# Attention's products with the values in a hybrid decoder layer: two parts of the values held stationary, two parts of the probabilities streamed

## The chip, the cores and the metric

The kernel runs on one core of a Trainium2 chip. A core has a matrix engine (TensorE, PE in the profile, with its weight loads listed as PEld), a vector engine (VectorE, DVE), a scalar engine (ScalarE, ACT), a general engine (GpSimd, POOL) and a sync engine (SyncE, SP) that here issues nearly all DMA transfers. Each engine has its own instruction queue and works through it in order; they wait for one another by semaphores. SBUF is the working memory, 128 partitions wide, and PSUM the memory into which TensorE writes its results. The metric is the device time of one execution in microseconds (us).

## The reference, cut to what matters

The layer projects the input, runs a gated linear recurrence and a sliding-window attention on the projections, merges both, and ends in a mixture of experts. The change touches the attention alone: 1024 tokens in 8 blocks of 128, 8 query heads and 2 key/value heads of width 64, a window of 128, a linear penalty on distance and one sink logit per head.

```
scores = einsum('bnqhgd,bnkhd->bnhgqk', qb, kb) * scale
logits = where(valid, scores - alibi, NEG_INF)        # own block and the block before
probs  = softmax(concatenate([logits, sink_col], -1), -1)[..., :-1]
out    = einsum('bnhgqk,bnkhd->bnqhgd', probs, vb)
```

Because the window is as wide as a block, each query sees exactly 128 keys: key c of its own block where c is not after the query, and key c of the block before where it is. The kernel therefore keeps one 128 x 128 table per head and block, filled from the one block or the other by a triangular mask.

## The kernel before, in words

All large products are float32 made of three products of a faster type (fp32r): an operand is split into a rounded part and the remainder (`split`, L96 to L98: ScalarE copies, VectorE subtracts), and `mm3` (L100 to L104) adds high x high, high x low and low x high. Attention's scores use two such products per head, since both parts of the queries lie on the two halves of the partitions (L337, L338). Its turning of the probabilities (L367), its products with the values (L381, L383) and the turning of its output (L406) use plain float32.

The work stands in stages. `att_proj` projects queries, keys and values. Then `weave` (L241) lays the pieces of `attention()` between the products of `stream()`, the remaining projections: 164 nominal us of projections are divided evenly by the number of attention's pieces, and that many products are fed before each piece. TensorE's order is this program order, fixed by `pe_order`; the other engines are ordered by the scheduler of the language. The next stage weaves the recurrence with the rest of the projections in the same manner, then come mixing and routing, and then the experts, whose weights SyncE fetches into a ring of buffers from the end of the mixing on.

For block n and half g of the heads (four heads), attention has three pieces, put into the list by the numbers in `groups` so that one group's pieces stand four places apart:

- `scores(n, g)`: eight products into the bank `sc`; ScalarE copies the own block's part (L341), VectorE overwrites the masked part from the block before (L345), adds the distance term (L350), takes the maximum (L352); ScalarE takes the exponentials (L360). `prep(n + 1)` is issued within the second group.
- `turn(n, g)`: four transposes into a bank `pa`; VectorE multiplies the result by the mask of the own block into `apc` (L369) and by the mask of the block before into `app` (L373).
- `values(n, g)`: per head `apc` is stationary and the values of the block stream, 64 columns and a 65th of ones that gives the sum of the exponentials (L381); for n > 0 the same with `app` and the block before (L383). VectorE adds the sink (L385), inverts (L386), and scales into `ob` (L387).

A fourth piece per block, `out(n)`, turns the block's output by four transposes (L406), copies it on ScalarE (L408) and stores it to DRAM (L409). The tiles named in `S2` (L68) share one ring of `n2` = 15 buffers, and the banks `mm` (3), `sc` (1) and `pa` (3) hold all of PSUM.

Of the kernel before, what the change touches and what calls it, by code (L numbers as in the profile page):

```python
# [5 lines left out]
F32 = mybir.dt.float32  # L6
F32R = mybir.dt.float32r
I32 = mybir.dt.int32
AF = mybir.ActivationFunctionType
# [51 lines left out]
class Builder:  # L61
# [3 lines left out]

    S2 = {"ob", "as", "apc", "app", "oT", "hq", "hk", "hl", "hv", "hg", "hkd", "hkT", "hqb", "hst", "hE", "hS", "hsq", "ho",  # L68
          "rxT", "rlT", "hh", "hth", "htl"}
    NQ = 36  # L70
    NX = 9
# [6 lines left out]
    def tile(self, shape, dt, tag, bufs, name=None):  # L78
        name = name or tag
        if tag in self.S2:  # L80
            tag, bufs = "s2", self.n2
# [160 lines left out]
    def att_proj(self):  # L242
        nc = self.nc
        self.xh, self.xl = [], []
        x0 = [self.load_x(0, 0)]
        raw = [self.wload_half(2048, 0)]
        x0.append(self.load_x(0, 1))
        raw.append(self.wload_half(2048, 1))
        x0 += [self.load_x(0, j) for j in (2, 3)]
        x1 = [self.load_x(1, j) for j in range(4)]  # L250
        raw2 = self.wload(2304)
        self.setup_more()
        raw3 = self.wload(2560)
        self.aq = [self.q4([128, 4, 256], name=f"aq{i}") for i in range(4)]

        def keep(ps, ch, ct, half):
            for b in range(2):
                nc.scalar.activation(self.aq[2 * half + b][:, 2 * ch + ct], ps[:, 256 * b:256 * b + 256], AF.Copy, scale=0.125)

        def query(w, ch, half):  # L260
            for ct in range(2):
                keep(self.run(self.proj_T(w, ct, half)), ch, ct, half)

        def first():

            w, xs = [], self.split_x(0, x0)
            gens = [self.proj_T(w, ct, 0) for ct in range(2)]
            for j in range(4):
                next(xs)
                if j % 2 == 0:  # L270
                    w.append(self.wsplit_half(raw[j // 2]))
                for _ in range(2):
                    for gen in gens:
                        next(gen)
            for ct, gen in enumerate(gens):
                keep(self.run(gen), 0, ct, 0)
            return w

        w = first()
        for _ in self.split_x(1, x1):  # L280
            pass
        query(w, 0, 1)
        w = self.wsplit(raw2)
        for half in range(2):
            query(w, 1, half)
        w = self.wsplit(raw3)
        self.ak = self.q4([128, T], name="ak")
        self.av = self.tile([128, 8, 2, 65], F32, "av", 1)
        nc.gpsimd.memset(self.av[:, :, :, 64:65], 1.0)
        self.ksh = self.tile([128, 2, 2, 128], F32R, "ksh", 1)  # L290
        self.ksl = self.tile([128, 2, 2, 128], F32R, "ksl", 1)
        vts = []
        for half in range(2):
            s = slice(half * 512, half * 512 + 512)
            ps = self.run(self.proj_T(w, 0, half))
            nc.scalar.copy(self.ak[:, s], ps)
            ps = self.run(self.proj_T(w, 1, half))
            vt = self.st2()
            nc.scalar.copy(vt, ps)
            vts.append(vt)  # L300
        for half, vt in enumerate(vts):
            tp = self.bank("pa", (128, 4, 128))
            for i in range(4):
                nc.tensor.transpose(tp[:, i], vt[:, i * 128:i * 128 + 128], self.c("ident"))
            nc.vector.tensor_copy(self.av[:, 4 * half:4 * half + 4, :, 0:64], tp.rearrange("p i (g d) -> p i g d", g=2))

    def attention(self):

        nc = self.nc
        lo, hi = slice(0, 64), slice(64, 128)  # L310
        V = {}

        def prep(n):
            o = (n % 2) * 128
            q = self.aq[n // 2]
            qs = self.tile([128, 2, 4, 128], F32R, "aqs", 2)
            nc.scalar.copy(qs[lo, 0], q[lo, :, o:o + 128])
            nc.scalar.copy(qs[hi, 1], q[hi, :, o:o + 128])
            nc.vector.tensor_sub(qs[hi, 0], q[lo, :, o:o + 128], qs[lo, 0].bitcast(F32))
            nc.vector.tensor_sub(qs[lo, 1], q[hi, :, o:o + 128], qs[hi, 1].bitcast(F32))  # L320
            cs = n % 2
            kb = slice(n * 128, n * 128 + 128)
            for g, own, other in ((0, lo, hi), (1, hi, lo)):
                nc.scalar.copy(self.ksh[own, g, cs], self.ak[own, kb])
                nc.scalar.copy(self.ksh[other, g, cs], self.ak[own, kb])
                for to in (own, other):
                    nc.vector.tensor_sub(self.ksl[to, g, cs], self.ak[own, kb], self.ksh[own, g, cs].bitcast(F32))
            V["qs", n] = qs
            V["ob", n] = self.tile([128, 8, 64], F32, "ob", 2)

        def scores(n, g):
            qs = V["qs", n]
# [6 lines left out]
            s = self.tile([128, 4, 128], F32, "as", 2)  # L339
# [8 lines left out]
            if g == 1 and n < 7:  # L348
                prep(n + 1)
# [4 lines left out]
            sk = self.tile([128, 4], F32, "ask", 2)  # L354
            nc.vector.tensor_sub(sk, self.sink[:, g::2], m)
            nm = self.tile([128, 4], F32, "anm", 2)
            nc.vector.tensor_scalar(nm, m, -1.0, None, op0=ALU.mult)
            nc.scalar.activation(sk, sk, AF.Exp)
            for i in range(4):
                nc.scalar.activation(s[:, i], s[:, i], AF.Exp, bias=nm[:, i:i + 1])  # L360
            V["s", n, g] = s, sk

        def turn(n, g):
            s, _ = V["s", n, g]
            pt = self.bank("pa", (128, 4, 128))
            for i in range(4):
                nc.tensor.transpose(pt[:, i], s[:, i], self.c("ident"))  # L367
            pc = self.tile([128, 4, 128], F32, "apc", 2)
            nc.vector.tensor_mul(pc, pt, self.c("le")[:, None, :].to_broadcast([128, 4, 128]))  # L369
            pp = None  # L370
            if n:
                pp = self.tile([128, 4, 128], F32, "app", 2)
                nc.vector.tensor_mul(pp, pt, self.c("gt")[:, None, :].to_broadcast([128, 4, 128]))  # L373
            V["p", n, g] = pc, pp

        def values(n, g):
            _, sk = V.pop(("s", n, g))
            pc, pp = V.pop(("p", n, g))
            o_ps = self.bank("pa", (128, 4, 65))
            for i in range(4):  # L380
                nc.tensor.matmul(o_ps[:, i], pc[:, i], self.av[:, n, i // 2], start=True, stop=not n)  # L381
                if n:
                    nc.tensor.matmul(o_ps[:, i], pp[:, i], self.av[:, n - 1, i // 2], start=False, stop=True)  # L383
            den = self.tile([128, 4, 1], F32, "ad", 2)
            nc.vector.tensor_add(den, o_ps[:, :, 64:65], sk[:, :, None])  # L385
            nc.vector.reciprocal(den, den)  # L386
            nc.vector.tensor_mul(V["ob", n][:, g::2], o_ps[:, :, 0:64], den.to_broadcast([128, 4, 64]))  # L387

        def out(n):
            self.out_T(V.pop(("ob", n)).rearrange("p h d -> p (h d)"), self.obd, n, "pa")  # L390

        prep(0)
        groups = []
        for n in range(8):
            for g in range(2):
                at = 8 * n + 4 * g
                groups += [(at, lambda n=n, g=g: scores(n, g)), (at + 5.5, lambda n=n, g=g: turn(n, g)),
                           (at + 10.6, lambda n=n, g=g: values(n, g))]
            groups.append((8 * n + 18.7, lambda n=n: out(n)))
        return [fn for _, fn in sorted(groups, key=lambda t: t[0])]  # L400

    def out_T(self, src, dst, n, tag):
        nc = self.nc
        ps = self.bank(tag, (128, 4, 128))
        for k in range(4):
            nc.tensor.transpose(ps[:, k], src[:, k * 128:k * 128 + 128], self.c("ident"))  # L406
        t = self.tile([128, 4, 128], F32, "oT", 3)
        nc.scalar.copy(t, ps)  # L408
        nc.sync.dma_start(dst.rearrange("k p t -> p k t")[:, :, n * 128:n * 128 + 128], t)  # L409


    def hg_consts(self):
# [1000 lines left out]
    def build(self):  # L1413
        pool = self.tc.tile_pool
        with pool(name="base", bufs=1) as self.base, pool(name="dr", bufs=1, space=DRAM) as self.dr:
            self.setup()
            self.n2 = 15
            self.banks = {"mm": 3, "sc": 1, "pa": 3}
            with pool(name="sb1", bufs=1, reuse_waits="tile") as self.sb, \
                    pool(name="ps1", bufs=1, space=PSUM, reuse_waits="tile") as self.ps, self.pe_order():  # L1420
# [6 lines left out]
            with pool(name="sb2", bufs=1, reuse_waits="tile") as self.sb, \  # L1427
                    pool(name="ps2", bufs=1, space=PSUM, reuse_waits="tile") as self.ps, self.pe_order():
                groups = self.hgrn()
# [58 lines left out]
```

## Time and profile before

Three runs took 1441.64, 1442.16 and 1442.84 us; the median is 1442.16. The profiled execution took 1442.8 us, of which the span from the first to the last instruction is 1441.0 us.

| stretch (us) | work | PE busy | DVE busy | ACT busy | POOL busy | DMA share |
|---|---|---|---|---|---|---|
| 80 to 306 | attention between projections | 226.00 of 226 | 130.40 | 102.36 | 0.52 | - |
| 306 to 420 | recurrence begins | 113.18 of 114 | 75.99 | 48.94 | 7.37 | 0.44 |
| 530 to 640 | recurrence ends, mixing begins | 107.99 of 110 | 69.68 | 35.50 | 22.87 | 0.55 |
| 640 to 760 | mixing and routing | 118.56 of 120 | 77.60 | 23.32 | 4.65 | 0.54 |
| 900 to 1050 | experts | 150.00 of 150 | 135.53 | 120.93 | 34.88 | 0.99 |

Busy time of PE is the time in which at least one matmul was in flight; their durations overlap, so what one costs is read from the distance between starts, not from its duration. A wait listed with an engine is idle time that ended when the named instruction was done.

### The profile page before, as it was taken

How to read it: one execution, taken by the hardware profiler on the slowest of the kernel's cores; microseconds unless marked ns; L12 is line 12 of the kernel's file. 1: busy time of each engine (PE TensorE's matmuls, PEld its weight loads, DVE VectorE, ACT ScalarE, POOL GpSimd, SP SyncE). 2: the span in 40 equal slices, each digit the busy share in tenths (PEclk: the TensorE clock that was granted, in tenths of full speed). 3: DMA queues.
4: the chain of work that ended last, by engine and by line, in shares of the span. 5: the costliest groups of instructions: out<-in, count | busy, mean ns of one | idle time of the engine just before them, and what ended most of it. 6: DMA issues, size and time to landing. Idle time of an engine off the chain costs nothing. (4 is left out here: it accounts for less than half of the span.)

```text
span 1441.0 us, 20557 instructions
## 1 busy us (share of the span) xinstructions
PE 1378.0 (96%) x7314; PEld 1147.4 (80%) x7314; DVE 1017.3 (71%) x1624; ACT 774.9 (54%) x1192; POOL 198.1 (14%) x133
## 2 busy tenths in 40 slices
PE   7999999999999999999999999999999999999844
PEld 5888899998888888788787888888888888888721
DVE  4266644646765764767746799999999999999635
ACT  4366434324443442422201688888888888888533
POOL 0000000000000000320001112222222222222123
PEclk9999999999999999999999999999999999999967
DMA  6123322344334232774466799999999999999962
GB/s 261 50 99 126 102 74 81 103 131 137 109 103 140 89 109 71 244 256 140 160 235 234 288 359 366 367 357 356 355 355 359 354 355 356 367 359 360 369 268 95
DMA packets 142555, 327.71 MB, mean 227 GB/s; under 512 B 18614, under 2 KB 59702, under 8 KB 142448
## 3 DMA queue, kind: packets, MB, share of 16 engines
q1 hardware_dynamic: 132800, 308.78, 59.4%
q0 software_dynamic: 9648, 17.57, 4.8%
q8 instruction: 59, 0.97, 0.3%
q14 instruction: 48, 0.39, 0.1%
HBM read 291.43 MB, written 52.43 MB: 239 GB/s over the span
## 5 line engine op out<-in xcount | busy, mean ns | idle before, releaser
L98 DVE TENSOR_TENSOR el<-er,eh 128x1024 fp32r<-128x1024 f32 x368 | 436.8, 1223 | 52.8 <-ACT eh L97 35.8
L97 ACT CAST eh<-er 128x1024 fp32r<-128x1024 f32 x368 | 369.2, 1053 | 99.4 <-PE mm L103 80.0
L102 PE MATMUL mm<-xh,wh 128*128 128x512 f32 x480 | 199.0, 415 | 8.3 <-ACT wh L97 7.3
L102 PE MATMUL mm<-eh,xh 128*128 128x512 f32 x496 | 196.4, 396 | 0.0
L103 PE MATMUL mm<-el,xh 128*128 128x512 f32 x496 | 196.2, 395 | 0.0
L104 PE MATMUL mm<-eh,xl 128*128 128x512 f32 x496 | 196.1, 395 | 0.0
L104 PE MATMUL mm<-xh,wl 128*128 128x512 f32 x480 | 189.1, 394 | 0.0
L103 PE MATMUL mm<-xl,wh 128*128 128x512 f32 x480 | 188.4, 393 | 0.8 <-DVE xl L98 0.8
L104 PEld LDWEIGHTS mm<-eh,xl 128*128 128x128 f32 x496 | 93.2, 188 | 22.6
L103 PEld LDWEIGHTS mm<-el,xh 128*128 128x128 f32 x496 | 93.2, 188 | 22.3
L102 PEld LDWEIGHTS mm<-eh,xh 128*128 128x128 f32 x496 | 93.2, 188 | 22.3
L102 PEld LDWEIGHTS mm<-xh,wh 128*128 128x128 f32 x480 | 91.1, 190 | 24.1 <-ACT wh L97 7.3
L104 PEld LDWEIGHTS mm<-xh,wl 128*128 128x128 f32 x480 | 90.7, 189 | 20.5 <-DVE wl L98 0.8
L103 PEld LDWEIGHTS mm<-xl,wh 128*128 128x128 f32 x480 | 91.2, 190 | 15.9 <-DVE xl L98 1.3
L102 PE MATMUL mm<-eh,hth 128*128 128x512 f32 x240 | 100.2, 417 | 0.0
L1054 POOL DMA_INDIRECT xg<-x1d,gi x32 | 58.0, 1811 | 282.8 <-PE pb L1117 266.8
L104 PE MATMUL mm<-eh,htl 128*128 128x512 f32 x240 | 94.8, 395 | 0.0
L103 PE MATMUL mm<-el,hth 128*128 128x512 f32 x240 | 94.8, 395 | 0.0
L1058 POOL DMA_INDIRECT zd<-y,gi x29 | 71.0, 2447 | 158.0 <-ACT y L1208 158.0
L102 PE MATMUL mm<-wh,xh 128*128 128x256 f32 x256 | 74.1, 290 | 0.0
L103 PE MATMUL mm<-wl,xh 128*128 128x256 f32 x256 | 72.4, 283 | 0.0
L104 PE MATMUL mm<-wh,xl 128*128 128x256 f32 x256 | 72.3, 282 | 0.0
(249 smaller groups left out, 2490.6 us busy)
## 6 DMA issues: line engine op xcount, KB each, us to landing
er<-w_g SPq DMA_DIRECT2D x128, 512.0 KB, 12.4
er<-w_u SPq DMA_DIRECT2D x128, 512.0 KB, 12.5
er<-w_d SPq DMA_DIRECT2D x128, 512.0 KB, 12.1
wr<-w_in SPq DMA_DIRECT2D x38, 512.0 KB, 4.1
gated<-st SPq DMA_DIRECT2D x32, 256.0 KB, 2.1
st<-gated SPq DMA_DIRECT2D x32, 256.0 KB, 3.3
xr<-xt SPq DMA_DIRECT2D x8, 512.0 KB, 8.9
wab<-w_a SPq DMA_DIRECT2D x16, 256.0 KB, 3.9
```

The costliest lines, as they stand in the source:

```text
L97: self.nc.scalar.copy(hi, src)
L98: (eng or self.nc.vector).tensor_sub(lo, src, hi.bitcast(F32))
L102: mm(out, lh, rh, start=start, stop=False)
L103: mm(out, lh, rl, start=False, stop=False)
L104: mm(out, ll, rh, start=False, stop=stop)
L1054: self.nc.gpsimd.indirect_dma_start(to, None, rows, bass.IndirectOffsetOnAxis(ap=self.column(self.gi, e), axis=0), bounds_check=T - 1, oob ...
L1058: self.nc.gpsimd.indirect_dma_start(self.zd, bass.IndirectOffsetOnAxis(ap=idx, axis=0), y, None, bounds_check=T - 1, oob_is_err=False, com ...
```

## The change

The values are kept in two parts, rounded and remainder, side by side: 64 columns of the one and 64 of the other make a stationary operand of 128 columns per block and key/value head. The probabilities are divided by their sum before they are turned; that sum is gathered by the exponentials themselves (`accum_out`). `turn` splits the turned probabilities into two parts, and for n > 0 masks each part for the own block on VectorE into a new tile and for the block before on GpSimd in place. In `values` the two heads of one key/value head stream together, 256 columns, in two parts. The result has the product with the rounded values on partitions 0 to 63 and that with their remainder on 64 to 127; ScalarE copies the latter down and VectorE adds. It then already has the layout that `out` made by transposes, so `out` goes, and attention has 48 pieces where it had 56. The ring `s2` has 13 buffers.

```diff
-        self.av = self.tile([128, 8, 2, 65], F32, "av", 1)
-        nc.gpsimd.memset(self.av[:, :, :, 64:65], 1.0)
+        self.av = self.tile([128, 8, 2, 2, 64], F32R, "av", 1)
...
-            nc.vector.tensor_copy(self.av[:, 4 * half:4 * half + 4, :, 0:64], tp.rearrange("p i (g d) -> p i g d", g=2))
+            av = self.av[:, 4 * half:4 * half + 4]
+            self.split(av[:, :, :, 0], av[:, :, :, 1], tp.rearrange("p i (g d) -> p i g d", g=2))
...
             nc.scalar.activation(sk, sk, AF.Exp)
+            den = self.tile([128, 4], F32, "ad", 2)
             for i in range(4):
-                nc.scalar.activation(s[:, i], s[:, i], AF.Exp, bias=nm[:, i:i + 1])
-            V["s", n, g] = s, sk
+                nc.scalar.activation(s[:, i], s[:, i], AF.Exp, bias=nm[:, i:i + 1], accum_out=den[:, i:i + 1])
+            nc.vector.tensor_add(den, den, sk)
+            nc.vector.reciprocal(den, den)
+            nc.vector.tensor_mul(s, s, den[:, :, None].to_broadcast([128, 4, 128]))
+            V["s", n, g] = s
...
-            pc = self.tile([128, 4, 128], F32, "apc", 2)
-            nc.vector.tensor_mul(pc, pt, self.c("le")[:, None, :].to_broadcast([128, 4, 128]))
-            pp = None
+            parts = [self.tile([128, 4, 128], F32R, nm, 2) for nm in ("aph", "apl")]
+            self.split(*parts, pt)
+            V["p", n, g] = [(n, parts)]
             if n:
-                pp = self.tile([128, 4, 128], F32, "app", 2)
-                nc.vector.tensor_mul(pp, pt, self.c("gt")[:, None, :].to_broadcast([128, 4, 128]))
-            V["p", n, g] = pc, pp
+                le, gt = (self.c(nm)[:, None, :].to_broadcast([128, 4, 128]) for nm in ("le", "gt"))
+                own = [self.tile([128, 4, 128], F32R, nm, 2) for nm in ("ach", "acl")]
+                for p, to in zip(parts, own):
+                    nc.vector.tensor_mul(to, p.bitcast(F32), le)
+                    nc.gpsimd.tensor_mul(p, p.bitcast(F32), gt)
+                V["p", n, g] = [(n, own), (n - 1, parts)]
...
-            o_ps = self.bank("pa", (128, 4, 65))
-            for i in range(4):
-                nc.tensor.matmul(o_ps[:, i], pc[:, i], self.av[:, n, i // 2], start=True, stop=not n)
-                if n:
-                    nc.tensor.matmul(o_ps[:, i], pp[:, i], self.av[:, n - 1, i // 2], start=False, stop=True)
-            den = self.tile([128, 4, 1], F32, "ad", 2)
-            nc.vector.tensor_add(den, o_ps[:, :, 64:65], sk[:, :, None])
-            nc.vector.reciprocal(den, den)
-            nc.vector.tensor_mul(V["ob", n][:, g::2], o_ps[:, :, 0:64], den.to_broadcast([128, 4, 64]))
-
-        def out(n):
-            self.out_T(V.pop(("ob", n)).rearrange("p h d -> p (h d)"), self.obd, n, "pa")
+            o_ps = self.bank("pa", (128, 4, 128))
+            todo = [(b, p) for b, parts in V.pop(("p", n, g)) for p in parts]
+            for j in range(2):
+                for k, (b, p) in enumerate(todo):
+                    nc.tensor.matmul(o_ps[:, 2 * j:2 * j + 2], self.av[:, b, j], p[:, 2 * j:2 * j + 2],
+                                     start=k == 0, stop=k == len(todo) - 1)
+            if g == 0:
+                V["o", n] = self.tile([128, 4, 128], F32, "oT", 3)
+            o = V["o", n][hi if g else lo]
+            low = self.tile([128, 4, 128], F32, "ob", 2)[lo]
+            nc.scalar.copy(low, o_ps[hi])
+            nc.vector.tensor_add(o, o_ps[lo], low)
+            if g:
+                self.store_T(V.pop(("o", n)), self.obd, n)
...
-            groups.append((8 * n + 18.7, lambda n=n: out(n)))
...
-            self.n2 = 15
+            self.n2 = 13
```

On TensorE, the first values piece of block 1 (`mm` is a bank of the projections, `pa` the bank of the result) stands in the order of before as

```order
L381 MATMUL pa_1016<-av_395,apc_879 128x65
L383 MATMUL pa_1016<-av_395,app_881 128x65
L381 MATMUL pa_1016<-av_395,apc_879 128x65
L383 MATMUL pa_1016<-av_395,app_881 128x65
L381 MATMUL pa_1016<-av_395,apc_879 128x65
L383 MATMUL pa_1016<-av_395,app_881 128x65
L381 MATMUL pa_1016<-av_395,apc_879 128x65
L383 MATMUL pa_1016<-av_395,app_881 128x65
L102 MATMUL mm_1006<-xh_204,wh_591 128x512
```

and in that of the change, whose lines from the attention on carry other numbers, as

```order
L104 MATMUL mm_1075<-xh_204,wl_596 128x512
L389 MATMUL pa_1085<-ach_928,av_395 128x256
L389 MATMUL pa_1085<-acl_929,av_395 128x256
L389 MATMUL pa_1085<-aph_924,av_395 128x256
L389 MATMUL pa_1085<-apl_925,av_395 128x256
L389 MATMUL pa_1085<-ach_928,av_395 128x256
L389 MATMUL pa_1085<-acl_929,av_395 128x256
L389 MATMUL pa_1085<-aph_924,av_395 128x256
L389 MATMUL pa_1085<-apl_925,av_395 128x256
L102 MATMUL mm_1075<-xh_204,wh_595 128x512
```

Eight products stand for eight, but 256 columns of the fast type for 65 of float32; the four rows `L406 MATMUL pa<-const,ob` per block have no successor.

On VectorE, around the scores of a later group (`as` is the table of scores, `am`, `ask`, `anm`, `ad` are columns of four, `st` belongs to a projection), before has

```order
L345 COPY_PREDICATED as<-const,sc 128x256 x2
L350 TENSOR_TENSOR as<-as,alibi 128x512
L352 TENSOR_REDUCE am<-as 128x4
L369 TENSOR_TENSOR apc<-pa,const 128x512
L353 TENSOR_TENSOR am<-am,sink 128x4
L373 TENSOR_TENSOR app<-pa,const 128x512
L357 TENSOR_SCALAR anm<-am 128x4
L462 TENSOR_SCALAR st_996<-st_996,om,lb 128x512
L385 TENSOR_TENSOR ad<-pa,ask 128x4
L355 TENSOR_TENSOR ask<-sink,am 128x4
L386 RECIPROCAL ad<-ad 128x4
L387 TENSOR_TENSOR ob<-pa,ad 128x4x64
```

and the change has

```order
L351 TENSOR_REDUCE am<-as 128x4
L352 TENSOR_TENSOR am<-am,sink 128x4
L354 TENSOR_TENSOR ask<-sink,am 128x4
L356 TENSOR_SCALAR anm<-am 128x4
L361 TENSOR_TENSOR ad<-ad,ask 128x4
L362 RECIPROCAL ad<-ad 128x4
L363 TENSOR_TENSOR as<-as,ad 128x512
L98 TENSOR_TENSOR apl<-pa,aph 128x512
L379 TENSOR_TENSOR ach<-aph,const 128x512
L379 TENSOR_TENSOR acl<-apl,const 128x512
L472 TENSOR_SCALAR st_1065<-st_1065,om,lb 128x512
L396 TENSOR_TENSOR oT<-pa,ob 64x512
```

The turn's work (`apl`, `ach`, `acl`) now stands behind the sum and the scaling (L361 to L363) of the group after it, where the two masks stood among the small steps before.

On GpSimd, which before had one fill (`av`) up to the recurrence's fill of `hst`, the change begins with

```order
L380 ISA
L380 TENSOR_TENSOR aph<-aph,const 128x512
L380 TENSOR_TENSOR apl<-apl,const 128x512
L380 TENSOR_TENSOR aph<-aph,const 128x512
L380 TENSOR_TENSOR apl<-apl,const 128x512
```

and has 28 of these masks, two for each of 14 groups.

## Rows read from the trace of the kernel before

**Rows 1.** The page: busy time and share of the span, TensorE.

```profile
PE 1378.0 (96%) x7314; PEld 1147.4 (80%) x7314; DVE 1017.3 (71%) x1624; ACT 774.9 (54%) x1192; POOL 198.1 (14%) x133
```

**Rows 2.** Busy time in 14 us stretches: stretch, its length, then each engine, clock, DMA.

```profile
94.40:108.80 14.40, 14.40 (x77) 12.23 (x76) 10.79 (x25) 10.72 (x25) 0.00 (x0) 1.00 0.39 131
...
236.00:250.00 14.00, 14.00 (x121) 14.00 (x120) 3.08 (x10) 4.14 (x13) 0.00 (x0) 1.00 0.18 57
...
sum 226.00, PE 226.00 PEld 209.79 DVE 130.40 ACT 102.36 POOL 0.52; mean PE 14.12 PEld 13.11 DVE 8.15 ACT 6.40 POOL 0.03
```

**Rows 3.** Waits of TensorE, 60 to 640 us: who waited, total us, times, longest.

```profile
PE mm L104 <- DVE l L98: 1.3, 3, 0.5
PE mm L102 <- ACT st L497: 0.7, 1, 0.7
PE pb L539 <- DMA hq<-hqd: 0.5, 1, 0.5
PE pb L573 <- DVE hE L559: 0.3, 1, 0.3
PE pa L304 <- ACT st L299: 0.2, 1, 0.2
```

**Rows 4.** Timeline of TensorE, a values piece of block 3: start, duration, line, operation.

```profile
180.13 0.34 PE L381 MATMUL pa<-av,apc 128*128 128x65 f32 x2
...
182.16 0.40 PE L103 MATMUL mm<-xl,wh 128*128 128x512 f32 x1
182.39 0.39 PE L104 MATMUL mm<-xh,wl 128*128 128x512 f32 x1
```

**Rows 5.** Timeline of TensorE, the turned output of block 2.

```profile
184.66 0.60 PE L406 MATMUL pa<-const,ob 128*128 128x128 f32 x4
...
185.33 0.39 PE L103 MATMUL mm<-xl,wh 128*128 128x512 f32 x1
```

**Rows 6.** Timeline of TensorE, a values piece of block 0.

```profile
98.88 1.00 PE L381 MATMUL pa<-av,apc 128*128 128x65 f32 x8
...
100.01 0.40 PE L103 MATMUL mm<-xl,wh 128*128 128x512 f32 x1
```

**Rows 7.** Timeline of TensorE, a scores piece: eight products of 256 columns.

```profile
188.52 0.28 PE L337 MATMUL sc<-ksh,aqs 128*128 128x256 f32 x1
...
189.48 0.39 PE L102 MATMUL mm<-xh,wh 128*128 128x512 f32 x1
```

**Rows 8.** Groups by line, 80 to 310 us: operands, count, busy us, mean ns, idle before.

```profile
L350 DVE TENSOR_TENSOR as<-as,alibi 128x512 f32<-128x512 f32 x16 | 11.1, 692 | 0.5
...
L369 DVE TENSOR_TENSOR apc<-pa,const 128x512 f32<-128x512 f32 x16 | 11.0, 684 | 0.7 <-PE pa L367 0.7
...
L387 DVE TENSOR_TENSOR ob<-pa,ad 128x256 f32<-128x256 f32 x16 | 6.8, 424 | 0.5
...
L408 ACT COPY oT<-pa 128x512 f32<-128x512 f32 x8 | 4.7, 587 | 23.0 <-PE pa L406 23.0
```

**Rows 9.** Line 1286, ScalarE's read of an accumulated sum: durations min/median/max in ns.

```profile
L1286 ACT ACTIVATION_READ_ACCUMULATOR w<-z x8: 185/187/198, 1386.6 to 1414.1; 128x1 f32 x8
```

**Rows 10.** Timeline of GpSimd at 582 us: one subtraction of 1024 columns.

```profile
582.70 2.40 POOL L98 TENSOR_TENSOR l<-wo,h 128x1024 fp32r<-128x1024 f32 x1 [15.31 <-PE mm L104]
```

**Rows 11.** Timeline of VectorE at the same time.

```profile
582.72 0.69 DVE L786 TENSOR_TENSOR st<-st,mm 128x512 f32<-128x512 f32 x1 [0.57 <-PE mm L104]
583.44 2.20 DVE L787 TENSOR_TENSOR st<-st,st 128x512 f32<-128x512 f32 x1
```

**Rows 12.** Timeline of ScalarE: exponentials of the first group and of the fourth.

```profile
85.77 1.28 ACT L360 ACTIVATE as<-as,anm 128x128 f32<-128x128 f32 x4
...
110.42 1.28 ACT L360 ACTIVATE as<-as,anm 128x128 f32<-128x128 f32 x4 [0.34 <-DVE anm L357]
```

**Rows 13.** Timeline of TensorE: the turns of the same two groups.

```profile
88.09 0.60 PE L367 MATMUL pa<-const,as 128*128 128x128 f32 x4
...
118.79 0.60 PE L367 MATMUL pa<-const,as 128*128 128x128 f32 x4
```

More of the change, by code (lines that the diff above doesn't have):

```diff
@@ L61 @@
 class Builder:
-    S2 = {"ob", "as", "apc", "app", "oT", "hq", "hk", "hl", "hv", "hg", "hkd", "hkT", "hqb", "hst", "hE", "hS", "hsq", "ho",
+    S2 = {"ob", "as", "aph", "apl", "ach", "acl", "oT", "hq", "hk", "hl", "hv", "hg", "hkd", "hkT", "hqb", "hst", "hE", "hS", "hsq", "ho",
           "rxT", "rlT", "hh", "hth", "htl"}
@@ L328, in prep @@
             V["qs", n] = qs
-            V["ob", n] = self.tile([128, 8, 64], F32, "ob", 2)
         def scores(n, g):
@@ L358, in scores @@
             nc.scalar.activation(sk, sk, AF.Exp)
+            den = self.tile([128, 4], F32, "ad", 2)
             for i in range(4):
-                nc.scalar.activation(s[:, i], s[:, i], AF.Exp, bias=nm[:, i:i + 1])
-            V["s", n, g] = s, sk
+                nc.scalar.activation(s[:, i], s[:, i], AF.Exp, bias=nm[:, i:i + 1], accum_out=den[:, i:i + 1])
[3 more added lines that the diff above has]
+            V["s", n, g] = s
         def turn(n, g):
-            s, _ = V["s", n, g]
+            s = V.pop(("s", n, g))
             pt = self.bank("pa", (128, 4, 128))
@@ L374, in turn @@
-            V["p", n, g] = pc, pp
-        def values(n, g):
-            _, sk = V.pop(("s", n, g))
-            pc, pp = V.pop(("p", n, g))
-            o_ps = self.bank("pa", (128, 4, 65))
-            for i in range(4):
-                nc.tensor.matmul(o_ps[:, i], pc[:, i], self.av[:, n, i // 2], start=True, stop=not n)
-                if n:
-                    nc.tensor.matmul(o_ps[:, i], pp[:, i], self.av[:, n - 1, i // 2], start=False, stop=True)
-            den = self.tile([128, 4, 1], F32, "ad", 2)
-            nc.vector.tensor_add(den, o_ps[:, :, 64:65], sk[:, :, None])
-            nc.vector.reciprocal(den, den)
-            nc.vector.tensor_mul(V["ob", n][:, g::2], o_ps[:, :, 0:64], den.to_broadcast([128, 4, 64]))
@@ L408, in out_T, with store_T @@
         nc.scalar.copy(t, ps)
-        nc.sync.dma_start(dst.rearrange("k p t -> p k t")[:, :, n * 128:n * 128 + 128], t)
+        self.store_T(t, dst, n)
+    def store_T(self, t, dst, n):
+        self.nc.sync.dma_start(dst.rearrange("k p t -> p k t")[:, :, n * 128:n * 128 + 128], t)
     def hg_consts(self):
```

## The prediction

> **What bounds the kernel now.** I read the page first: TensorE is in flight for 96% of the span, no other engine above 80% [rows 1]. That is an average, so next came the stretch that the change touches, cut into 14 us pieces. From 80 to 306 us TensorE is busy for all of 226.00 us, VectorE for 130.40, ScalarE for 102.36, GpSimd for 0.52 [rows 2]. VectorE's load is uneven: 10.79 us of 14.40 among the first projections, 3.08 of 14.00 at the low point. Third, the waits: over 60 to 640 us TensorE stands still for five reasons, 3.0 us in all, and none is a piece of attention [rows 3]; the nearest are the turn of the values before the first scores (0.2, L304) and the first product of the recurrence after the stage (0.5, L539). So in this stage TensorE's own products are the time, and a product less is time less, as long as what feeds it keeps its distance. I took the starts of the products from the timeline, since durations of 0.39 us overlap at distances of 0.23 us.
>
> **What TensorE loses and gains.** A values piece of a later block starts at 180.13 and the second product after it at 182.16; less the one ordinary distance of 0.23 (182.16 to 182.39) it costs 1.80 us [rows 4]. This includes a longer step to the first product after it, which both float32 pieces show and the scores do not. Fourteen such pieces: 25.2 us. The new piece is eight products of 256 columns of the fast type with a stationary operand of 128 columns. That is the form of a scores piece, 188.52 to 189.48, 0.96 us, 0.12 each [rows 7]. Fourteen: 13.4. Block 0 has two pieces of 100.01 - 98.88 - 0.23 = 0.90 us [rows 6], and gets two of four products, 0.48. The turned output is 185.33 - 184.66 - 0.23 = 0.44 us, eight times, and goes entirely [rows 5]. The sum is 11.8 + 0.8 + 3.5 = 16.1 us. The price of a product lies between 0.12 and the 0.23 of a 512-column one; at the upper end the 120 new products would cost 13 us more and the gain would be 3. I take 0.12, because the row has the same columns, type and operand size. A gain beyond it could come only from the load of weights being shared by neighbours, for which no row speaks.
>
> **What the other engines get.** VectorE, per group with n > 0: away go two masks of 0.68 and the scaling of 0.42; the two small steps on the sum remain. New are a subtraction from PSUM, two masks, a scaling of the table and a sum over 64 partitions, each priced by the rows of 512 columns at 0.69 [rows 8]. That is 3.45 for 1.79, some 1.66 more, 26.6 us over sixteen groups if block 0 is counted in full: 157 of the 210 us that TensorE would need. ScalarE, per group: a copy of the turned table and one of 64 partitions at about 0.59 each, by the output's copy [rows 8], half of which per group goes; four reads of the sums at 0.187 [rows 9]: 1.6 us, 26 in all, 128 of 210. At the start the two split copies of the values replace two copies. GpSimd: 28 masks of 512 columns. Before has no such operation; a subtraction of 1024 columns takes 2.40 us there [rows 10], so the bounds are 1.20 by columns and 2.40 if nothing of it scales; I take 1.20, since the size differs and the kind doesn't. All of this lies beside TensorE and costs nothing while the distance holds.
>
> **What distance there is.** From the end of the exponentials to the turn: for the fourth group 111.7 to 118.8, 7.1 us [rows 12, 13]; the new steps in between, four reads, sum, inverse and scaling, take about 0.7 + 0.2 + 0.2 + 0.7 = 1.8. VectorE must now wait at the sum (L361) until ScalarE has read the last accumulator; behind it stand the split and the masks of the turn before, then a step of a projection. For them wait GpSimd's masks and with them TensorE's next values piece, and ScalarE's next activation of that projection. That chain (copy, subtraction, two masks, GpSimd's two) is about 0.6 + 0.7 + 0.7 + 0.7 + 2.4, with the steps between engines some 6 us, and a values piece stands four pieces behind its turn: about 13 us, for a group takes a sixteenth of the stage. Two places are closer. The first group's exponentials end at 87.05 and its turn starts at 88.09, 1.0 us [rows 12, 13]. The wider spacing of the pieces (164/48 for 164/56) puts three more products, 0.7 us, before that turn, against 1.8 us of new steps and the split of the values ahead of them: I book a stall of 0.5, between 0 and 2. The last turn has, in the new order, 60 products of 256 columns and one values piece before the last values piece, 60 x 0.12 + 0.96, about 8.2 us against a chain of 6 to 7.5: 0.3 booked, between 0 and 1.5. At the border to the recurrence the same projections end last as before. The expert weights are fetched by SyncE behind the stores of the mixing, so their stream moves with the rest.
>
> **The forecast.** 16.1 - 0.8 = 15.3 us. The profiled execution took 1442.8 us, 1.8 more than its span, and would take 1427.5; it stands 0.6 over the median, so the median should be 1426.9, say 1427.
>
> [...] Beside GpSimd's 2.40 us a subtraction of one table and one bank stays at 0.69 us, while the sum of two tables lasts 2.20 and ends 0.5 us after GpSimd does [rows 10, 11]. [...]
>
> **Rivals.** First, stalls in the dense part: VectorE and ScalarE are at 10.8 and 10.7 us of 14.4 there [rows 2], and with 1.7 and 1.6 more per group, the wait at L361 (1.3 to 2 us while ScalarE works on exponentials) and some blocking by GpSimd, VectorE has 14 to 15 us of work in a cycle of 13.4. It would fall behind by 1 us a group and use up the 5 us of distance left; then some pieces of the first half wait, 0.5 us in each of 12: 6 us, 1433. For it speaks the load, against it that the mean of the stage is far lower and that only the groups of block 1 meet the heaviest projections with masks on GpSimd.
>
> Second, on the other side: VectorE becomes the bound of the whole stage. Its place is the sum of two tables beside a GpSimd mask. If each of 28 masks blocks VectorE by the most that the rows show, 2.20 - 0.69 = 1.5 us, that is 42 us; the wait for the exponentials adds 16 x 1.6 = 26. With 157 us of work this is 225, and if VectorE, in order as it is, keeps a tenth of the 96 us for which it idled before (226 - 130), the stage lasts 235 where it lasted 226: 1451. It decides from the point where VectorE's stage passes 226 us. [...]
>
> Third, no change: the gain is hidden, because the stretch from 900 to 1350 us runs with DMA engines nearly full, and its end is set by the weights. That needs the stream of weights to start at a time that attention does not set. Its issues stand behind the mixing's stores in one queue, which speaks against it; time 1442.
>
> **Chances.** The forecast, 1424.5 to 1430: 0.72. First rival, 1430 to 1439: 0.14. Second, above 1445: 0.07. Third: 0.07. What a measurement of this kernel can tell from no change is about 0.2%, 2.9 us. The first two cases are faster by more than that, 0.86; the third is 0.07 same, the second 0.07 slower. The range from 1424 to 1434 holds the first case and about half of the first rival: 0.8.
>
> **What would show it.** In the profile after: values pieces of 0.96 us from start to start, and no turned output; the stage from the first scores to the recurrence's first product about 15 us shorter; in the waits of TensorE at most a microsecond or two at turns (by VectorE's scaling, L363) or values (by GpSimd, L380), at the start and at the end of the stage. GpSimd's masks about 1.2 us each; VectorE's masks `ach`, `acl` or scaling stretched beyond 0.69 where they meet. Wrong it would be if the values products stood 0.2 us apart, if TensorE waited for L380 or L363 in group after group, or if a stage behind the attention grew by what this one lost.

## The result and the profile after

The changed kernel takes 1424.03 us, the median of 4 runs (1422.8 to 1425.84); the kernel before took 1442.5 beside it, the median of 4. The ratio is 0.9866 with a 95% interval from 0.9851 to 0.9881: 17 to 21.5 us less. Forecast were 1427 and a gain of 15.3; the gain is about 3 us larger. The time lies 0.5 us under the forecast's case of 1424.5 to 1430. Of the wider range, 1424 to 1434, it just meets the lower end; taken as a ratio to the kernel before it lies below that end, 0.9866 against the 0.9874 that 1424 is of the earlier median of 1442.16. The profiled execution took 1423.78 us.

The page again, its line of busy times (against [rows 1]):

```profile
PE 1359.1 (96%) x7162; PEld 1128.3 (79%) x7162; DVE 1058.2 (74%) x1654; ACT 792.3 (56%) x1282; POOL 239.6 (17%) x160
```

The attention stage in the same stretches as [rows 2]: length, then PE, PEld, DVE, ACT, POOL, the granted clock, DMA share and GB/s.

```profile
94.40:108.80 14.40, 14.40 (x73) 12.09 (x72) 10.23 (x25) 11.30 (x31) 0.00 (x0) 1.00 0.40 127
...
137.60:152.00 14.40, 14.08 (x72) 11.69 (x71) 13.86 (x28) 9.14 (x24) 3.20 (x2) 1.00 0.33 111
...
236.00:250.00 14.00, 14.00 (x120) 14.00 (x119) 8.59 (x17) 7.85 (x21) 2.83 (x2) 1.00 0.34 109
...
sum 226.00, PE 225.39 PEld 206.85 DVE 178.25 ACT 124.74 POOL 43.52; mean PE 14.09 PEld 12.93 DVE 11.14 ACT 7.80 POOL 2.72
```

VectorE's load went from 130.40 to 178.25 us and reaches 13.86 of 14.40 in one stretch, where TensorE, full elsewhere up to the last stretch, lost 0.32 us. Before, that stretch was among VectorE's fullest too, with 11.21 where the prediction took 10.79 for the dense part:

```profile
137.60:152.00 14.40, 14.40 (x82) 12.44 (x81) 11.21 (x25) 7.24 (x16) 0.00 (x0) 1.00 0.28 92
```

TensorE's waits from 60 to 640 us (against [rows 3]):

```profile
PE mm L104 <- DVE l L98: 2.2, 5, 0.5
PE mm L102 <- ACT st L507: 0.7, 1, 0.7
PE pa L371 <- DVE as L363: 0.3, 1, 0.3
PE pb L549 <- issue: 0.3, 1, 0.3
PE pa L303 <- ACT st L298: 0.2, 1, 0.2
```

In the attention's stage the change brought one wait, that of a turn for the scaling (L363), 0.3 us; nothing waits for GpSimd's masks (L380), and the waits for `l` (L98) all lie behind the stage. The wait is not where 0.5 was booked: the first turn, at 88.75 us, had none. It is the sixth of the sixteen turns, in the stretch where VectorE is fullest:

```profile
150.50 0.63 PE L371 MATMUL pa<-const,as 128*128 128x128 f32 x4 [0.32 <-DVE as L363]
```

Ahead of that scaling, two of VectorE's steps took 1.53 and 1.68 us beside two of GpSimd's masks; without such masks the same lines take 0.42 and 0.69 on the mean (a_vmask below).

```profile
144.67 1.53 DVE L515 TENSOR_SCALAR st<-st 128x512 f32<-128x512 f32 x1
146.22 1.68 DVE L320 TENSOR_TENSOR aqs<-aq,aqs 64x512 fp32r<-64x512 f32 x1
...
149.65 0.69 DVE L363 TENSOR_TENSOR as<-as,ad 128x512 f32<-128x512 f32 x1
```

```profile
144.15 1.76 POOL L380 TENSOR_TENSOR aph<-aph,const 128x512 fp32r<-128x512 f32 x1 [9.89 <-DVE ask L354]
145.87 1.47 POOL L380 TENSOR_TENSOR apl<-apl,const 128x512 fp32r<-128x512 f32 x1
```

A values piece on TensorE's timeline (against [rows 4] and [rows 7]; the next product after it stands at 278.69):

```profile
277.75 0.28 PE L389 MATMUL pa<-ach,av 128*128 128x256 f32 x1
277.87 0.28 PE L389 MATMUL pa<-acl,av 128*128 128x256 f32 x1
...
278.57 0.28 PE L389 MATMUL pa<-apl,av 128*128 128x256 f32 x1
278.69 0.28 PE L102 MATMUL mm<-wh,xh 128*128 128x256 f32 x1
```

Eight products 0.12 us apart, 0.94 in all: the price taken from the scores.

Where the time went is read from the starts of the same lines in both profiles:

| stretch | before | after | difference |
|---|---|---|---|
| first scores to the recurrence's first product (L539, now L549) | 241.7 | 226.3 | -15.4 |
| to the recurrence's last output (L622, now L632) | 243.1 | 242.5 | -0.6 |
| to the mixing's last gate (L785, now L795) | 157.0 | 158.2 | +1.2 |
| to the last transposes of routing (L921, now L931) | 63.3 | 63.3 | 0 |
| to the first product on gathered rows (L1117, now L1127) | 22.5 | 18.9 | -3.6 |
| to the first scaled row of the experts (L1208, now L1218) | 34.0 | 34.0 | 0 |
| to the last one | 508.7 | 507.4 | -1.3 |
| to the end of the span | 91.3 | 92.0 | +0.7 |

The attention gave what was forecast, 15.4 for 15.3. The rest comes almost all from one place without any attention in it, the end of routing. There stands a branch (L1345, now L1355), and every engine steps over it. The line in the profile before (queue, operation, count, ns min/median/max, first and last start in us):

```profile
L1345 DVEq COMPARE_BRANCH  x1: 72/72/72, 802.9 to 802.9; - x1
...
L1345 PEldq COMPARE_BRANCH  x1: 518/518/518, 803.1 to 803.1; - x1
...
L1345 PEldq EVENT_SEMAPHORE  x1: 51/51/51, 804.7 to 804.7; - x1
L1345 DVEq EVENT_SEMAPHORE  x1: 21/21/21, 806.8 to 806.8; - x1
```

and in the profile after:

```profile
L1355 PEldq COMPARE_BRANCH  x1: 353/353/353, 787.0 to 787.0; - x1
L1355 DVEq COMPARE_BRANCH  x1: 72/72/72, 787.1 to 787.1; - x1
...
L1355 PEldq EVENT_SEMAPHORE  x1: 51/51/51, 787.5 to 787.5; - x1
...
L1355 DVEq EVENT_SEMAPHORE  x1: 21/21/21, 787.7 to 787.7; - x1
```

VectorE's queue needs 3.9 us from the branch to its release before, 0.6 after. What TensorE makes of it: its last dummy products and the first product on gathered rows, before

```profile
798.43 6.21 PE L115 MATMUL mm<-const 128*128 128x128 f32 x40
806.96 1.06 PE L1117 MATMUL pb<-const,xg 128*128 128x128 f32 x8 [2.32 <-DVEq L1345]
```

and after

```profile
782.42 4.71 PE L115 MATMUL mm<-const 128*128 128x128 f32 x40
788.47 1.07 PE L1127 MATMUL pb<-const,xg 128*128 128x128 f32 x8 [1.33 <-DMA xg<-x1d,gi]
```

Two things differ. TensorE waits for VectorE's release in one, for the gathered rows in the other; and the same 40 passes take 6.21 us against 4.71. The second is the granted clock (the column before the DMA share), which fell to 0.50 in before:

```profile
792.00:794.00 2.00, 0.60 (x6) 0.60 (x6) 1.86 (x12) 0.55 (x2) 0.00 (x0) 1.00 1.02 418
794.00:796.00 2.00, 2.00 (x15) 2.00 (x14) 1.86 (x14) 2.00 (x3) 0.00 (x0) 0.69 1.03 422
796.00:798.00 2.00, 2.00 (x10) 1.83 (x10) 0.81 (x5) 0.48 (x1) 0.00 (x0) 0.50 1.02 410
```

after a stretch in which TensorE was busy for 0.60 of 2 us; in after it stayed at 1.00 through the same work.

### The profile page after: what moved, and what is told of

The parts are those of the page before. It is cut to its first block, busy times and chain, and to the rows that moved or that the text cites. A ratio compares the mean times of both kernels' runs of the same rounds, so it can differ in the third digit from the quotient of the medians.

```text
span 1421.9 us, 20450 instructions
## 1 busy us (share of the span) xinstructions
PE 1359.1 (96%) x7162; PEld 1128.3 (79%) x7162; DVE 1058.2 (74%) x1654; ACT 792.3 (56%) x1282; POOL 239.6 (17%) x160
## 5 line engine op out<-in xcount | busy, mean ns | idle before, releaser
L98 DVE TENSOR_TENSOR el<-er,eh 128x1024 fp32r<-128x1024 f32 x368 | 436.5, 1221 | 53.7 <-ACT eh L97 38.1
```

What stands on the lines that cost most here:

```text
L98: (eng or self.nc.vector).tensor_sub(lo, src, hi.bitcast(F32))
```

## The experiments

Three theories for the 3 us behind the attention: the granted clock alone (1), an effect of attention's new pattern on what follows (2), the place of the branch in VectorE's code (3, formed after the first four runs). Starts of lines are compared as in the table above; "routing to gathered" is its fifth row.

**More dummy products in routing's gaps**, in before (b_warm) and after (a_warm):

```diff
-    WARM = {63: 11, 65: 5, 66: 14, 67: 5}
+    WARM = {63: 13, 65: 5, 66: 20, 67: 7}
```

> The kernel before, with more dummy products in the gaps of routing (13, 5, 20, 7 of them at ticks 63, 65, 66, 67 instead of 11, 5, 14, 5). Theory 1, the clock: the change gains about 15.5 us in attention, and the other 3 to 3.5 us come from the granted clock, which fell to 0.50 at the end of routing in before and did not in after. If the dummies hold the clock at 1.00 there, the kernel before takes 1438.5 to 1439.5 us instead of 1442. Theory 2, a true effect of the change behind the attention (weights, queues, engines that run ahead): the kernel before stays at 1442 to 1443, whatever the clock at routing does.

Measured 1443.23 us (ratio to before 1.0001, 0.9991 to 1.0011). The clock held at 1.00 up to 804 us, and nothing was gained: VectorE's step at the branch took 4.1 us, TensorE waited 4.08 for it (2.32 in before), and behind that standstill the clock fell (0.50 at 806 us). So the clock alone does not explain the difference.

> The changed kernel with the same larger number of dummy products at routing. Its granted clock was 1.00 there already. Theory 1: nothing to gain, 1423.5 to 1425 us, and the distance to the kernel before with the same dummies is 14.5 to 15.5 us, as forecast for the attention alone. Theory 2: the distance stays at 18 us.

1425.49 us (0.9871, 0.9851 to 0.9891), no gain either; the step took 0.6 us, and TensorE waited 1.94 for the gathered rows.

**Every values product twice** (a_twice):

```diff
-            for j in range(2):
+            for j in (0, 1, 0, 1):
                 for k, (b, p) in enumerate(todo):
```

> The changed kernel with every product of the probabilities with the values issued twice (the second pass starts its sum anew, so the result is unchanged): 120 products more. If a product costs 0.12 us, as forecast, the stage from the first scores to the recurrence's first product grows by 14.4 us (120 x 0.12); if the price were 0.23, by 27.6; if the pieces were hidden behind VectorE or GpSimd, by much less. The total by theory 1: +14.4 us if the granted clock at routing stays at 1.00, 17.5 to 18 if it falls as in before, since routing then starts at nearly the time at which it starts in before. By theory 2: +14.4.

1439.83 us. The stage grew from 226.3 to 240.2, 13.9 for 120 products: 0.116 each. The price is on TensorE's path, as forecast. The whole time is 15.8 above after, between the totals that theories 1 and 2 gave, and settles neither. In the profiled execution the clock fell in routing (0.50 at 796 us; 0.982 on the mean of the span, 0.986 in after), and routing to gathered took 20.7.

**The saved time given back as dummy products** behind the attention (a_fill):

```diff
                 self.weave(self.attention(), stream, 164)
+                self.warm(66)
```

> The changed kernel with 66 dummy products (132 passes at 0.118 us, 15.5 us) of TensorE put between attention and recurrence, which give back the whole time that the change saves there, so that routing starts at the time at which it starts in before. Theory 1, if it is the time at which routing comes that decides on the clock: the clock falls again and the total is 1442 to 1443 us, 18.5 above after. If the total is 1439.5 (+15.5) with a clock of 1.00 at routing, it is not the time alone that decides. Theory 2, an effect of the change that the fill does not undo: 1439.5 too, but with the same lead at routing's end whatever the clock.

1439.83 us, 15.8 above after. The stage took 240.8, routing to gathered 19.3 at a clock of 1.00 (0.986 on the mean of the span, as in after), the step at the branch 0.6 us. Routing came 2.5 us earlier than in before, so the time at which it comes was nearly the same, and yet its end was 3.2 us shorter: the time at which routing comes does not decide.

**The branch moved in VectorE's code.** In the compiled program the branch is VectorE's instruction 1334 in before, and 1376 after, since the change gives VectorE 42 instructions more ahead of it (the traces hold 1329 and 1371 records of VectorE ahead of the branch). Fills of one column at the start move it (b_dve42; a_dve86 with 86, b_dve21 and b_dve84 alike):

```diff
-        nc.vector.memset(self.negc, NEG)
+        for _ in range(43):
+            nc.vector.memset(self.negc, NEG)
```

> The kernel before with 42 more tiny fills on VectorE at the very start, while it waits for the first transfer, so that the branch at the end of routing (L1345) stands at the same place in VectorE's instructions as in the changed kernel, which has 42 more of them. The profiles show that VectorE needs 3.9 us from that branch to its release in before and 4.1 with more dummies, but 0.6 in all four profiles of the changed kernel, and that TensorE's first gathered product waits for it. Theory 3, the place of the branch in VectorE's code: here the step takes 0.6 us, TensorE waits for the gathered rows instead, and the time is 1.5 to 2.5 us lower, 1440 to 1441. Theory 1, the granted clock alone: the step stays at 4 us and the time at 1442.3. Theory 2, an effect of attention on what follows: the same, no change.

1440.36 us, ratio 0.9982 (0.9971 to 0.9992): faster, with more work. The step took 0.6 us:

```profile
L1346 DVEq COMPARE_BRANCH  x1: 72/72/72, 803.7 to 803.7; - x1
...
L1346 DVEq EVENT_SEMAPHORE  x1: 21/21/21, 804.3 to 804.3; - x1
```

Routing to gathered went from 22.5 to 19.6. TensorE now waited 2.01 us for its own step over the branch (1.79 us in its queue). The fills were not free: the first scores came 1.8 us later.

> The changed kernel with 86 more tiny fills on VectorE at the start, so that the branch stands 128 instructions behind its place in before, which is the same place in a block of 128 instructions (the trace moves instructions of that queue in blocks of 8 KB). Theory 3: VectorE's step from branch to release takes about 4 us again, TensorE's first gathered product waits for it, and the time is 1.5 to 2.5 us above after, 1425.5 to 1427. Theories 1 and 2: 0.6 us and no change, 1424 to 1425.

1434.58 us. The step took 3.9 us again, TensorE waited 3.93 for it, routing to gathered took 21.5 for 18.9, and the clock fell behind it (0.50 at 798 us; 1.6 us more to the first scaled row). The size can't be read from the whole time: the fills lasted 0.124 us each, 10.8 in all, and the first scores came 5.8 us later; 1434.58 is far above the 1425.5 to 1427 that theory 3 gave.

> The kernel before with 21 tiny fills more on VectorE at the start: the branch at the end of routing stands halfway between its place in before (3.9 us to the release) and in the changed kernel (0.6 us). Theory 3: one of the two values, 0.6 or about 4 us, and none between; the time 1440 to 1442.5 accordingly.

The branch at 1355: 0.6 us; the time 1440.99 (one run).

> The kernel before with 84 tiny fills more on VectorE at the start (their own length delays the start by some 5 us): the branch stands 42 instructions behind its place in the changed kernel. Theory 3: the step from branch to release is again 0.6 or about 4 us; with blocks of 128 instructions it need not be that of the changed kernel. If it were a matter of how much VectorE does ahead, and not of the place, it would be 0.6 as with 42.

At 1418: 0.6 us; the time 1448.52 (one run). The first scores came 4.3 us later by the fills, and the mixing took 3.8 more, which is not explained.

**The same without a delay at the start**: fills between the steps of the mixing, 86 in after (a_slow) and 42 in before (b_fast), into a new tile `dummy` of one column:

```diff
+            if 4 <= tick < 47:
+                for _ in range(2):
+                    self.nc.vector.memset(self.dummy, 0.0)
             self.warm(self.WARM.get(tick, 0))
```

> The changed kernel with 86 tiny fills on VectorE, two after each of 43 steps of the mixing, so that the branch stands at the same place in a block of 128 instructions as in before. Theory 3: the step takes 3.9 us, TensorE stands still for 4 us where it waited 1.3, and the clock may fall behind the standstill, as it did in a_dve86 and with more dummies in before: 2.5 to 4.5 us above after, 1426.5 to 1428.5, which is what was forecast for the change without this. Theory 1 (the clock alone) and theory 2: 1423.5 to 1425.

1431.9 us, above the range that theory 3 gave. Step and wait are as it says:

```profile
L1359 DVEq COMPARE_BRANCH  x1: 72/72/72, 788.7 to 788.7; - x1
...
L1359 DVEq EVENT_SEMAPHORE  x1: 21/21/21, 792.7 to 792.7; - x1
```

```profile
792.83 1.71 PE L1131 MATMUL pb<-const,xg 128*128 128x128 f32 x8 [4.07 <-DVEq L1359]
```

Routing to gathered 21.6 (+2.7), the next stretch 35.7 (+1.7, the clock again, 0.50 at 794 us). Of the other 3.9 of the profile's 8.3 us most lie in the mixing (1.9, beside the fills) and among the experts (1.9, not explained).

In before one fill after each of 42 steps:

```diff
+            if 4 <= tick < 46:
+                for _ in range(1):
+                    self.nc.vector.memset(self.dummy, 0.0)
             self.warm(self.WARM.get(tick, 0))
```

> The kernel before with 42 tiny fills on VectorE, one after each of 42 steps of the mixing: the branch stands where it stands in the changed kernel. Theory 3: the step takes 0.6 us and the time is 2 to 3.5 us lower, 1439 to 1440.5; then the change alone, at equal places of the branch, is worth 15 to 16.5 us. Theories 1 and 2: 1442 to 1443.

1442.13 us beside 1443.17 for before: 0.999 (0.9981 to 0.9999), 1.4 us less by the ratio, fewer than expected. The step took 0.6, routing to gathered 19.3 for 22.5. Lost elsewhere in that profile: 1.7 by the first scores, where the clock fell at 24 to 28 us (0.50 and 0.65), and 0.8 among the experts.

**GpSimd's masks on VectorE** (a_vmask), the second rival's question:

```diff
-                    nc.gpsimd.tensor_mul(p, p.bitcast(F32), gt)
+                    nc.vector.tensor_mul(p, p.bitcast(F32), gt)
```

> The changed kernel with the masks of the block before on VectorE in place of GpSimd: 28 masks of 0.69 us more on VectorE (19 us), and no GpSimd work beside it. If GpSimd blocks VectorE in this stage and TensorE's distance is as large as forecast, both cost TensorE nothing: first scores to the recurrence's first product stays at 226.3 us within 0.5, and VectorE's tables of 512 columns (the scaling, 0.80 us on the mean, and a projection's step, 0.91) fall back to 0.69 and 0.43. If VectorE is close to the bound, the stage grows by up to 19 us.

1426.19 us in one run, with a fall of the clock in routing (0.50 at 780 to 786 us; 20.4 to gathered). The stage took 226.1 for 226.3, without a wait at a turn or a values piece, and VectorE was busy for 176.98 us of 226, not more than with the masks on GpSimd (178.25). Groups by line in the changed kernel, 80 to 310 us (busy us, mean ns):

```profile
L380 POOL TENSOR_TENSOR aph<-aph,const 128x512 fp32r<-128x512 f32 x14 | 22.8, 1627 | 247.7 <-DVE ach L379 184.0 <-ACT as L360 31.5 <-ACT ob L395 13.4
...
L380 POOL TENSOR_TENSOR apl<-apl,const 128x512 fp32r<-128x512 f32 x14 | 20.3, 1453 | 0.0
L515 DVE TENSOR_SCALAR st<-st 128x512 f32<-128x512 f32 x16 | 14.5, 906 | 1.4 <-ACT st L514 1.3
...
L363 DVE TENSOR_TENSOR as<-as,ad 128x512 f32<-128x512 f32 x16 | 12.7, 796 | 0.5
...
L320 DVE TENSOR_TENSOR aqs<-aq,aqs 64x512 fp32r<-64x512 f32 x6 | 6.1, 1016 | 0.2
...
L361 DVE TENSOR_TENSOR ad<-ad,ask 128x4 f32<-128x4 f32 x16 | 5.6, 350 | 18.9 <-ACT as L360 18.9
```

and with the masks on VectorE:

```profile
L363 DVE TENSOR_TENSOR as<-as,ad 128x512 f32<-128x512 f32 x16 | 11.1, 691 | 0.5
...
L380 DVE TENSOR_TENSOR aph<-aph,const 128x512 fp32r<-128x512 f32 x14 | 9.6, 686 | 0.0
L380 DVE TENSOR_TENSOR apl<-apl,const 128x512 fp32r<-128x512 f32 x14 | 9.6, 686 | 0.0
...
L515 DVE TENSOR_SCALAR st<-st 128x512 f32<-128x512 f32 x16 | 6.8, 423 | 3.0 <-ACT st L514 2.9
...
L320 DVE TENSOR_TENSOR aqs<-aq,aqs 64x512 fp32r<-64x512 f32 x6 | 4.1, 688 | 0.2
...
L361 DVE TENSOR_TENSOR ad<-ad,ask 128x4 f32<-128x4 f32 x16 | 2.6, 163 | 17.8 <-ACT as L360 17.7
```

The stretched steps of these four lines (16 x 0.48 at L515, 16 x 0.11 at L363, 6 x 0.33 at L320, 16 x 0.19 at L361) come to 14.4 us. Over the whole stage, VectorE's work other than the 28 masks is 157.8 us here (176.98 less 19.2) and 178.25 with the masks on GpSimd, 20.5 more. Moving them off VectorE had freed nothing.

**GpSimd's masks twice** (a_pool2):

```diff
-                    nc.gpsimd.tensor_mul(p, p.bitcast(F32), gt)
+                    for _ in range(2):
+                        nc.gpsimd.tensor_mul(p, p.bitcast(F32), gt)
```

> The changed kernel with each of GpSimd's 28 masks done twice (the second changes nothing). In the profile of the changed kernel GpSimd's masks take 43 us and VectorE is busy for 178 of 226 us, as much as with the masks on VectorE itself (177), so what GpSimd takes is added to instructions of VectorE. If that blocking goes on, VectorE comes to 205 to 215 us of busy time, TensorE begins to wait for masks (L380) or the scaling (L363) in some groups of the first half, and the stage grows by 0.5 to 6 us. If TensorE's distance is large enough, it grows by less than 0.5; if VectorE becomes the bound, by 10 us or more.

1434.4 us in one run. The stage took 238.7, 12.4 more; VectorE's busy time in it grew by 15.4. VectorE came to 193.7 of 237 us, short of the 205 to 215 expected, and yet the stage lost more than the 10 us that were expected only if VectorE became the bound. TensorE's waits, 60 to 640 us:

```profile
PE pa L371 <- DVE as L363: 8.1, 3, 3.8
...
PE pa L390 <- POOL apl L381: 0.4, 1, 0.4
```

Three turns wait for the scaling, up to 3.8 us; the clock fell behind two of these standstills (0.50 at 182 us, 0.54 at 292). GpSimd busy for 91 us in the stage is too much; for 43.5 it came with one wait of 0.3.

**The turned output put back** (a_turnout), with a constant in place of the output:

```diff
+        def spare():
+            ps = self.bank("pa", (128, 4, 128))
+            for k in range(4):
+                nc.tensor.transpose(ps[:, k], self.c("ident"), self.c("ident"))
+
...
+            groups.append((8 * n + 18.7, spare))
```

> The changed kernel with the eight turned outputs put back as four transposes of a constant each, which nobody reads: the same products of TensorE at the same places of the row of pieces as in before, and no other engine in it. By the forecast this costs 8 x 0.44 = 3.5 us of the 16.1: first scores to the recurrence's first product 229.8 us for 226.3, and the time 1427 to 1428. If the turned output was worth less (its transposes hidden behind waits), the stage stays nearer to 226.3 and the price of the values pieces has to be more than forecast.

1428.27 us, ratio to before 0.9904 (0.9888 to 0.9921). The stage took 230.3, 4.0 more than after: about the 3.5 of the forecast, and a wait of 0.7 at one turn.

**The changed kernel again** (a_again), without an edit.

> The changed kernel once more, for a second profile and more times. Theory 3: VectorE's step at the branch again 0.6 us. Theory 1 asks how often the granted clock falls in routing; the time is 1423 to 1426 whether it falls or not, 1 to 2 us higher where it does.

1423.45 us (2 runs), the step 0.6, routing to gathered 19.1.

## Why the prediction was right about attention and short by 3 us

- **What bounds it, right.** TensorE's products are the time of the stage: 120 more of them lengthen it by 13.9 (a_twice), eight turned outputs by 4.0 (a_turnout).
- **The sum for TensorE, right.** 16.1 less 0.8 of stalls was forecast, 15.4 measured; the products' price was 0.116 for 0.12. The stalls were booked in the wrong places: 0.5 at the first turn and 0.3 at the last pieces, where none came; the 0.3 that did come stood at the sixth turn. With that alone the sum would have been 15.8, so part of the agreement is luck.
- **GpSimd's masks, under-sized.** 1.20 us was taken between 1.20 and 2.40; beside a busy VectorE they last 1.63 and 1.45, 43 us for 34.
- **VectorE, under-sized, without a price.** 157 us were forecast, 178 measured; without masks on GpSimd the same work takes 157.8 (a_vmask), so nearly the whole miss is what GpSimd's masks add. The second rival took that at 1.5 us a mask, 42 in all; it was 20.5, and VectorE did not become the bound. The rows had shown the sum of two tables stretched (2.20 us beside GpSimd's 2.40, [rows 10, 11]); the most stretched step here is a projection's with a single table (L515, 0.91 us for 0.42).
- **The distance, right but smaller than it looked.** The first rival's mechanism is real: with twice the masks three turns wait and the stage loses 12.4. With the masks as they are it cost one turn 0.3, in the first half of the stage, where this rival looked.
- **"Their stream moves with the rest", the step that failed.** All behind the attention was taken to move unchanged, so the sum had no term there. Between the last transposes of routing and the first gathered product 3.6 us went. VectorE's step over the branch took 3.9 to 4.1 us in the four profiles where the branch is instruction 1334 or 1462, and 0.6 in all twelve where it is 1355, 1376 to 1379, 1390 or 1418, with old attention or new. To the experts' first scaled row the four take 56.5 to 57.3 us from the last transposes; the others 52.9 to 53.7 where the clock stayed at 1.00 and 54.4 to 54.8 in the three where it fell. In before the clock fell ahead of the branch, so of the 3.6 about 2 are the place of the branch, and the rest is the clock in that execution. In the other three the clock fell behind the wait instead, and place and fall together make 3.4 to 4.4.

Shown is that the place decides on VectorE's step, in both directions and with either attention. Not settled is its worth in whole times: b_dve42 and b_fast give 2.6 and 1.4 us by their ratios, a_slow 7.9 by the medians (5.9 by the ratios to before) with other losses in it, because fills cost something too. Open stay why the clock falls in routing in some kernels and not in others, and why the experts' stretch varies between 507.3 and 509.5.

As to the cause of the long step, the page lists the transfers of instructions (here of the changed kernel):

```profile
q14 instruction: 49, 0.40, 0.1%
```

That is 8 KB in each of 49. The DMA view of single stretches tells when they came. In before, none came from 765.1 us to the branch, and these three between the branch (802.92) and VectorE's release (806.84), all under way within 2.3 us of the branch:

```profile
q14 instruction: 3, 0.02, 1.5%
```

In after one came from 778 us to the branch (787.06), and none between the branch and the release (787.65):

```profile
q14 instruction: 1, 0.01, 0.2%
```

All sixteen profiles fall into these two kinds. In the four with the long step the last such block had come 37 to 38 us ahead of the branch, and three or four blocks started before the release; in the twelve with the short step one had come 4 to 22 us ahead, and the next started 1.3 to 1.9 us after the branch, behind the release. The two slow places, 1334 and 1462, are 128 instructions apart, which fits a block of 128. An estimate from the page of before comes near that: of its 20557 instructions 14628 are TensorE's products and loads, and if its 48 blocks hold the other 5929, that is 124 each. So what sets the two kinds apart is a block in the last 22 us ahead of the branch, which is missing where the step is long. That VectorE then waits for such a block is still an inference, since the transfers do not tell which engine they are for.

No run points to a kernel that is better than the changed one: there the step is short already, and more dummies or masks on VectorE gained nothing.

## What to carry to other kernels

Where one engine is full and no other sets a wait, count its products from start to start and trust the sum; then ask how far each helper is from the point where it turns late, since here doubling the work of an engine used for 43 of 226 us cost 12.4. A change of the number of instructions moves every later branch in that engine's code, and here 42 idle fills made a kernel 1.4 to 2.6 us faster; so compare the steps over branches in both profiles before a difference in a stage that wasn't touched is put down to the change. Moving 28 masks from VectorE to GpSimd was no relief here (VectorE was busy for 178.25 us against 176.98): before counting on such a move, compare VectorE's busy time with and without it.

## What was not expected of the hardware

- VectorE's step over the branch took 0.6 or 3.9 to 4.1 us in sixteen profiles, and nothing between, by the place of the branch in the code. TensorE's own step, in its queue, took 0.23 to 1.79 us.
- With 28 masks of 128x512 on GpSimd VectorE is as busy (178.25 us) as when it does them itself (176.98).
- A fill of one column on VectorE took 0.124 us, so 42 of them are 5.2 us.
- The granted clock fell to 0.50 for 3.4 to 6.8 us in routing in some executions and not in others with the same work there; it cost 1 to 2 us.
